# Two feed-forwards whose activations are turned by the DMA: another order of writes in the copy ahead of it, and a later place for the transposes

## The chip, the cores and the metric

The kernel runs on one core of one Trainium2 chip. The metric is the device time of an execution in microseconds; the number to compare is the median of the runs. One execution is also recorded by the profiler, and every figure of a trace below is from that one.

## The reference, cut to what matters

A block of two layers on 256 tokens of width 2048, in float32: layer 0 mixes with differential attention, layer 1 with a state-space scan, and each ends in a gated feed-forward of 5,632 hidden columns, modulated by a vector made from `c`.

```python
for i in range(DEPTH):                     # DEPTH = 2
    ada = c_act @ ada_w[i] + ada_b[i]      # shift, scale and gate, twice
    ...
    x = x + gate1 * m                      # m: attention (layer 0) or scan (layer 1)
    h = rms_norm(x, norm2_g[i]) * (1.0 + scale2) + shift2
    x = x + gate2 * swiglu(h, ffn_w_gate_up[i], ffn_w_down[i])

def swiglu(h, w_gate_up, w_down):
    g, u = jnp.split(h @ w_gate_up, 2, axis=-1)
    return (jax.nn.silu(g) * u) @ w_down
```

The change is in what lies between the two products of `swiglu`: silu(g) * u comes out with tokens on the partitions, and the second product needs hidden columns there, so it must be transposed.

## The kernel before, in words

**Units.** Weights are read from HBM once, in units of 256 rows by 512 columns (512 KB). `split_unit` (line 249) issues a unit's load on SP's queue into one of seven buffers `raw` (L253), ScalarE (ACT) casts it to `wh`, the high part (L256), and VectorE (DVE) subtracts to get `wl`, the low part. TensorE (PE) then does 12 matmuls of 512 columns: two 128-row tiles, two blocks of 128 tokens, three products of high and low parts. There are four buffers of `wh` and `wl`, so the cast of a unit waits for PE to finish the unit four before it, and the load for a `raw` buffer that the subtraction has freed. The helper that records PE's and DVE's instructions has line 120 in all rows.

**Order.** Nothing reorders instructions: each engine and each queue runs them as the program writes them. `push_unit` puts a unit's products into a first-in, first-out list, up to four units behind the loads; when a unit is taken out, its products are written, and then `tick` (line 198) lets other work advance. That work is in generators in the list `active`; `step_all` (line 179) runs each to its next `yield`, once per unit, so a `yield` is a distance of one unit. `flush_steps` (line 221) runs them all to their ends at once.

**Jobs.** The modulation vectors of later stages are computed beside all this: a job loads 512 KB of `ada_w` into the same seven `raw` buffers (L436), and DVE multiplies and adds it into `acc`. In layer 0's feed-forward 0.65 to 0.7 jobs are started per unit; in layer 1's there are hardly any in the second half of the first product.

**The feed-forward** (`ffn`, line 1328) goes in chunks j = 0 to 10 of 512 hidden columns, a gate and an up half each. Of chunks 0 to 4 and of chunk 5's up half the first half of the rows was summed and put aside in tiles `part` before the second half of the input was known. From then on a chunk takes 8 units (chunks 5, 0, 1, 2, 3 and 4, in that order; 4 for the gate, 4 for the up half) and then 16 (chunks 6 to 10). When an up half is done, `up_done` (line 1369) multiplies it on DVE into `sg`, one tile of 128 tokens by 512 columns for each of two blocks b, and starts `rest`:

- `halfwords` (L368): ACT takes each 4-byte word of `sg` apart into its two 2-byte halves, low halves in the tile's first 512 places, high halves in the second. Its loop runs over the words and within one over the halves, so that the writes go to and fro between the two places, 1,024 bytes apart.
- `turn` (L374): a DMA issued by SP transposes that tile, 128 partitions by 1,024 halves.
- `words` (L379): ACT puts the turned halves together again, in order of the result, in the tile `aT` that the second product reads. I call this the words copy.

There are 22 chunks in the two layers and two blocks in each, so 44 of each of these. The chain through `rest` is written unit by unit: one copy, a unit later the other, two units later both transposes, four units later the first words copy. Since SP issues loads and transposes from one queue, what stands behind a transpose waits while it waits for its copy.

After chunk 10 comes the down-projection, 88 units; ahead of its third column chunk, four units in, `call(flush_steps)` empties the generators (line 1468), what is left of chunk 10's `rest` among them.

Of the kernel before, what the change touches and what calls it, by code (L numbers as in the profile page):

```python
# [15 lines left out]
U16 = mybir.dt.uint16  # L16
# [14 lines left out]
RAW_BUFS = 7  # L31
W_BUFS = 4
RIPE = 1
PACE = 4
N_EARLY = 6
EPI = 3
# [55 lines left out]
def block_kernel(ctx: ExitStack, tc: tile.TileContext, x, x_t, columns_in, ssd_columns, da_columns, ada_w, ada_b,  # L92
# [13 lines left out]
    pe, act, dve, pool, sp = nc.tensor, nc.scalar, nc.vector, nc.gpsimd, nc.sync  # L106
# [65 lines left out]
        free[what] += n  # L172

    active = []
    pending = deque()
    gap = {"n": 0}
    hurry = []

    def step_all():
        for g in list(active):  # L180
            if next(g, StopIteration) is StopIteration:
                active.remove(g)
        gap["n"] -= 1
        if pending and gap["n"] <= 0 and pending[0][0]():
            _, g, n = pending.popleft()
            gap["n"] = n
            if next(g, StopIteration) is not StopIteration:
                active.append(g)
# [9 lines left out]
    def tick():  # L198
        while ripe and ripe[0][0] <= 0:
            ripe.popleft()[1]()  # L200
        for r in ripe:
            r[0] -= 1
        ada["acc"] = min(ada["acc"] + ada["rate"], 4.0)
        for k in ("dve", "dma"):
            load[k] = max(load[k], load["pe"] - 4000.0)
        while ada["acc"] >= 1.0 and len(jobs) > ada.get("floor", 0) and room():
            jobs.popleft()()
            ada["acc"] -= 1.0
        if not jobs:
            ada["acc"] = 0.0  # L210
        step_all()
# [9 lines left out]
    def flush_steps():  # L221
        while active or pending:
            step_all()

    def step_until(gen):
        while gen in active:
            step_all()
# [136 lines left out]

    def halfwords(src, p):

        h = p.tile([128, 2, 512], U16, tag="halfwords", name="halfwords", bufs=3)
        act.copy(h.rearrange("p e f -> p f e"), src.bitcast(U16).rearrange("p (f e) -> p f e", e=2))  # L368
        return h

    def turn(h, p):

        t = p.tile([128, 8, 128], U16, tag="turned", name="turned", bufs=3)
        sp.dma_start_transpose(t, h.rearrange("p e f -> p (e f)"))  # L374
        return t

    def words(dst, t):

        act.copy(dst.bitcast(U16).rearrange("p k (t e) -> p k t e", e=2),  # L379
                 t.rearrange("p (e k) t -> p k t e", e=2))  # L380
# [42 lines left out]
    def ada_job(layer, vec, finish, gate=False, halves=(0, 1)):  # L423
# [3 lines left out]
        def unit(hf, k):  # L427
            def run():
# [9 lines left out]
                def use():  # L438
# [7 lines left out]
                    if k == last:  # L446
                        acc = st["acc"]
                        ripe.append([1, lambda: finish(acc, hf)])
                ripe.append([RIPE, use])
            return run  # L450
# [84 lines left out]
    class Norm:  # L535
# [26 lines left out]
        def finish(self, b, q, on_act=False, later=False):  # L562

            ps = self.ps.pop((b, q))
            hm = tmp("hm")
            if q not in self.whole:
                self.whole[q] = act_tiles()
                self.h[q] = blocks(self.whole[q])
            h, l = self.h[q][b]
            hm3 = hm.rearrange("p (k t) -> p k t", k=4)  # L570
            for a in range(2):
                for i in (2 * a, 2 * a + 1):
                    k = 4 * q + i
                    o, p = hm3[:, i, :], ps[:, i * 128:(i + 1) * 128]
                    if on_act:
                        act.activation(o, p, AF.Identity, bias=self.Tm[:, k:k + 1], scale=self.S[:, k:k + 1])
                    else:
                        dve.tensor_scalar(o, p, self.S[:, k:k + 1], self.Tm[:, k:k + 1],
                                          op0=ALU.mult, op1=ALU.add)
            for a in range(2):  # L580
                k2 = slice(2 * a, 2 * a + 2)
                act.copy(h[:, k2, :], hm3[:, k2, :])

            def low():
                for a in range(2):
                    k2 = slice(2 * a, 2 * a + 2)
                    dve.tensor_tensor(l[:, k2, :], hm3[:, k2, :], h[:, k2, :].bitcast(F32), op=ALU.subtract)
            if later:
                return low
            low()  # L590
# [561 lines left out]
    for hg in range(4):  # L1152
        for qb, heads in ((0, (0, 1, 2, 3)), (1, (0, 1)), (1, (2, 3))):
            pending.append((lambda hg=hg: index[hg, 0] in ready and index[hg, 1] in ready,
                            attend(hg, qb, heads), PACE))

# [171 lines left out]
    def ffn(layer, end, first_jobs, final):  # L1328
        key = f"f{layer}"
        st = {}  # L1330
        top, low = ExitStack(), ExitStack()
# [13 lines left out]
        def slot(i, name):  # L1345

            return st["top" if i < 5 or i == 10 else "low"].tile([128, 4, 256], F32, tag=f"slot{i}", name=name)
# [21 lines left out]
        def up_done(j, bk, sg, i=None):  # L1369
            for b in range(2):  # L1370
                u = bk()[b]
                if i is not None:
                    dve.tensor_tensor(part[i][b], u, part[i][b], op=ALU.add)
                    u = part[i][b]
                dve.tensor_tensor(sg[b], sg[b], u, op=ALU.mult)

            def rest():
                yield
                turned = []
                for b in range(2):  # L1380
                    turned.append(halfwords(sg[b], st["top"]))
                    yield
                yield
                turned = [turn(h, st["top"]) for h in turned]
                for _ in range(4):
                    yield
                t = slot(10 if j == 5 else j if j < 5 else j - 1, f"aT_{j}")
                for b in range(2):
                    words(t[:, :, b * 128:(b + 1) * 128], turned[b])
                    yield  # L1390
                aT[j] = t
            active.append(rest())

        hl = {}

# [30 lines left out]
        sg = []  # L1426
        call(lambda bk=bk, sg=sg: gate_done(bk, sg))
        call(lambda: ada.update(rate=FFN_RATES[layer][1]))
        for i, (j, v) in [(10, (5, 1))] + list(enumerate(lead))[:10]:
            bk = Banks()  # L1430
            norm.push(wgu, v * F + j * 512, 512, bk, qs=(2, 3))
            if v == 0:
                sg = []
                call(lambda bk=bk, sg=sg, i=i: gate_done(bk, sg, i))
            else:
                call(lambda j=j, bk=bk, sg=sg, i=i: up_done(j, bk, sg, i))
        call(lambda: ada.update(rate=len(jobs) / 70))
        for j in range(6, 11):
            sg = []
            bk = Banks()  # L1440
            norm.push(wgu, j * 512, 512, bk)
            call(lambda bk=bk, sg=sg: gate_done(bk, sg))
            bk = Banks()
            norm.push(wgu, F + j * 512, 512, bk, after=(lambda: split(0)) if j == 10 else None)
            call(lambda j=j, bk=bk, sg=sg: up_done(j, bk, sg))
            if layer == 0 and j in (6, 8):
                call(ssd_load if j == 6 else ssd_finish)
# [488 lines left out]
```

## Time and profile before

| | us |
|---|---|
| median of 3 runs (2706.62 to 2714.54) | 2706.7 |
| the profiled execution's own time | 2713.09 |
| its span in the trace | 2711.4 |
| PE busy | 2637.8 |
| DVE busy | 1946.9 |
| ACT busy | 1574.1 |
| 44 copies at L368 | 214.9 |

The page gives busy time by engine, the costliest groups of instructions with the idle time ahead of them and what ended it, and the chain of work that ended last. "Busy" on PE counts a matmul from its start to its end while the next one is already in the array, so a start-to-start distance in the timeline says more of PE's pace than its busy share. In a table by stretch the granted clock is that of TensorE, with 1.00 for full speed. SPq is SP's queue, from which nearly all loads are issued.

### The profile page before, as it was taken

The page shows a single profiled execution, that of the slowest core. Times are in us where ns is not written, and L with a number is a line of the kernel's source. Part 1 is how long each engine was busy: PE and PEld are TensorE (multiplying, and loading weights), DVE is VectorE, ACT ScalarE, POOL GpSimd, SP SyncE. Part 2 cuts the span into 40 slices and gives each one's busy share as a digit, 9 for nine tenths or more (in the row PEclk, how much of TensorE's full clock was granted, in tenths as well). Part 3 has the DMA queues.
Part 4 walks back from the last instruction along what each step waited for, and adds up shares of the span by engine and source line. Part 5 has one row for each costly group of instructions (what it writes and reads, how often), then busy time and mean ns, then how long its engine had stood idle before and what let it go on. Part 6 is the DMA issues. An engine that isn't in the chain of part 4 may idle for free.

```text
span 2711.4 us, 35573 instructions
## 1 busy us (share of the span) xinstructions
PE 2637.8 (97%) x13072; PEld 2172.1 (80%) x13072; DVE 1946.9 (72%) x2263; ACT 1574.1 (58%) x1978; POOL 202.0 (7%) x205
## 2 busy tenths in 40 slices
PE   8999999999889999999999999999999999999999
PEld 4667778788667777888999989988888777887887
DVE  6778888777677876777777777776687554446776
ACT  4356754556765665445646566565545787666443
POOL 0024320001001210001000010010000000000001
PEclk9999999999999999999999999999999999999999
DMA  9977788698789987885566666666687555747885
GB/s 394 382 278 241 270 284 316 251 313 296 263 288 330 312 329 247 286 287 193 173 219 228 213 235 233 211 229 190 194 330 283 166 179 190 253 157 266 294 288 185
DMA packets 240464, 696.60 MB, mean 257 GB/s; under 512 B 68785, under 2 KB 77345, under 8 KB 239009
## 3 DMA queue, kind: packets, MB, share of 16 engines
q1 hardware_dynamic: 238560, 692.47, 72.7%
q8 instruction: 102, 1.67, 0.3%
q0 software_dynamic: 864, 1.62, 0.2%
q14 instruction: 74, 0.60, 0.1%
q10 hardware_dynamic: 864, 0.24, 0.0%
HBM read 680.52 MB, written 2.19 MB: 252 GB/s over the span
## 4 chain that ended last, share of the span: by engine, by line
PE 75%; DMA 7%; ACT 7%; DVE 6%; issue 4%; POOL 1%; SPq 0%; ACTq 0%; DVEq 0%; POOLq 0%
PE mm L120 58%; PE wk L120 13%; DMA raw<-in_ffn_w_gate_up 6%; PE po L120 4%; ACT halfwords L368 3%; ACT wh L256 3%; DVE wl L120 2%; DVE acc L120 2%; DVE sg L120 0%; DMA raw<-in_ffn_w_down 0%; DVE res L120 0%; DVE x L120 0%; DMA araw<-in_ada_w 0%; DMA raw<-in_ssd_w_in 0%; DMA cw<-in_ssd_columns 0%
## 5 line engine op out<-in xcount | busy, mean ns | idle before, releaser
L256 ACT CAST wh<-raw 128x1024 fp32r<-128x1024 f32 (+2 forms) x894 | 936.5, 1055 | 945.1 <-PE mm L120 517.7
L120 DVE TENSOR_TENSOR wl<-raw,wh 128x1024 fp32r<-128x1024 f32 (+2 forms) x894 | 1097.2, 1237 | 496.4 <-ACT wh L256 493.3
L120 PE MATMUL mm<-wh,ah 128*128 128x512 f32 (+1 forms) x2560 | 1021.1, 399 | 22.9 <-ACT wh L256 16.3
L120 PE MATMUL mm<-wl,ah 128*128 128x512 f32 (+1 forms) x2560 | 1008.6, 394 | 23.3 <-DVE wl L120 22.6
L120 PE MATMUL mm<-wh,al 128*128 128x512 f32 (+1 forms) x2560 | 1003.4, 392 | 0.1
L120 PEld LDWEIGHTS mm<-wh,ah 128*128 128x128 f32 x2560 | 484.2, 189 | 157.1 <-ACT wh L256 27.8
L120 PEld LDWEIGHTS mm<-wl,ah 128*128 128x128 f32 x2560 | 484.9, 189 | 140.0 <-DVE wl L120 42.9
L120 PEld LDWEIGHTS mm<-wh,al 128*128 128x128 f32 x2560 | 484.3, 189 | 102.1 <-DVE al L120 1.4
L120 DVE SCALAR_TENSOR_TENSOR acc<-raw,cT,acc 128x1024 f32<-128x1024 f32 x300 | 384.1, 1280 | 0.4
L368 ACT COPY halfwords<-sg 128x1024 uint16<-128x1024 uint16 x44 | 214.9, 4884 | 1.4 <-DVE sg L120 1.4
L120 PE MATMUL wk<-wl,ah 128*128 128x512 f32 x360 | 140.3, 390 | 1.3 <-DVE wl L120 1.3
L120 PE MATMUL wk<-wh,ah 128*128 128x512 f32 x360 | 140.2, 389 | 0.0
L120 PE MATMUL wk<-wh,al 128*128 128x512 f32 x360 | 140.1, 389 | 0.0
L120 PE MATMUL mm<-ah,wh 128*128 128x256 f32 x720 | 118.8, 285 | 0.0
L120 PE MATMUL mm<-al,wh 128*128 128x256 f32 x720 | 117.7, 283 | 0.0
L120 PE MATMUL mm<-ah,wl 128*128 128x256 f32 x720 | 117.6, 283 | 0.0
L530 POOL PARTITION_ALL_REDUCE gate<-acc x12 | 41.4, 3491 | 953.1 <-DVE acc L120 946.5
L120 PEld LDWEIGHTS mm<-ah,wh 128*128 128x128 f32 x720 | 100.2, 192 | 0.1
L120 PEld LDWEIGHTS mm<-ah,wl 128*128 128x128 f32 x720 | 100.2, 192 | 0.0
L120 PEld LDWEIGHTS mm<-al,wh 128*128 128x128 f32 x720 | 100.2, 192 | 0.0
L120 PEld LDWEIGHTS wk<-wl,ah 128*128 128x128 f32 x360 | 67.6, 188 | 16.2 <-DVE wl L120 2.2
L120 PEld LDWEIGHTS wk<-wh,ah 128*128 128x128 f32 x360 | 67.6, 188 | 14.2 <-ACT wh L256 0.3
(308 smaller groups left out, 2068.7 us busy)
## 6 DMA issues: line engine op xcount, KB each, us to landing
raw<-in_ffn_w_gate_up SPq DMA_DIRECT2D x352, 512.0 KB, 5.4
raw<-in_ada_w SPq DMA_DIRECT2D x320, 512.0 KB, 5.2
raw<-in_ffn_w_down SPq DMA_DIRECT2D x176, 512.0 KB, 5.1
raw<-in_ssd_w_in SPq DMA_DIRECT2D x136, 512.0 KB, 4.6
raw<-in_da_w_in SPq DMA_DIRECT2D x90, 512.0 KB, 5.3
araw<-in_ada_w SPq DMA_DIRECT2D x64, 512.0 KB, 8.5
raw<-in_ssd_w_out SPq DMA_DIRECT2D x64, 512.0 KB, 4.4
raw<-in_da_w_out SPq DMA_DIRECT2D x32, 512.0 KB, 5.3
```

The lines of the kernel that those rows point to most:

```text
L120: return fn(dst, *a, **k)
L256: act.copy(wh[:, at, :n], raw[:, at, :n])
L368: act.copy(h.rearrange("p e f -> p f e"), src.bitcast(U16).rearrange("p (f e) -> p f e", e=2))
L530: pool.partition_all_reduce(mods["G", key][:, o:o + 512], acc[:, i * 512:(i + 1) * 512], 128, ReduceOp.add)
```

## The change

Three things are different.

1. `halfwords` writes its tile in order: first all 512 low halves, then all 512 high ones. It reads every other half of `sg` for that. The same halves end in the same places.
2. `rest` lets six units (`LOADS_AHEAD`) pass after the second copy, then issues the transposes one by one, a unit apart, and two units later the words copies. From copy to transpose it was two units; it is now seven from either copy to its own transpose. From a transpose to its words copy it stays four. `halfwords` and `turned` have four buffers each for three.
3. `rest` is put into a list of its own, `apart`. `step_all` steps it after `active`, but `flush_steps` no longer runs until it is empty.

```diff
+LOADS_AHEAD = 6
...
     def step_all():
-        for g in list(active):
-            if next(g, StopIteration) is StopIteration:
-                active.remove(g)
+        for gs in (active, apart):
+            for g in list(gs):
+                if next(g, StopIteration) is StopIteration:
+                    gs.remove(g)
...
-        h = p.tile([128, 2, 512], U16, tag="halfwords", name="halfwords", bufs=3)
-        act.copy(h.rearrange("p e f -> p f e"), src.bitcast(U16).rearrange("p (f e) -> p f e", e=2))
+        h = p.tile([128, 2, 512], U16, tag="halfwords", name="halfwords", bufs=4)
+        act.copy(h, src.bitcast(U16).rearrange("p (f e) -> p e f", e=2))
...
-        t = p.tile([128, 8, 128], U16, tag="turned", name="turned", bufs=3)
+        t = p.tile([128, 8, 128], U16, tag="turned", name="turned", bufs=4)
...
             def rest():
                 yield
+                halves = []
+                for b in range(2):
+                    halves.append(halfwords(sg[b], st["top"]))
+                    yield
+                for _ in range(LOADS_AHEAD):
+                    yield
                 turned = []
-                for b in range(2):
-                    turned.append(halfwords(sg[b], st["top"]))
+                for h in halves:
+                    turned.append(turn(h, st["top"]))
                     yield
-                yield
-                turned = [turn(h, st["top"]) for h in turned]
-                for _ in range(4):
+                for _ in range(2):
                     yield
...
-            active.append(rest())
+            apart.append(rest())
```

Lines 368, 374, 379, 253, 256, 359 and 436 of before are 371, 377, 382, 256, 259, 362 and 439 after it.

SP's queue in layer 0, at the first transposes (chunk 5). Before:

```order
L436 DMA raw<-in_ada_w 128x1024
L253 DMA raw<-in_ffn_w_gate_up 128x1024
L436 DMA raw<-in_ada_w 128x1024
L253 DMA raw<-in_ffn_w_gate_up 128x1024
L374 DMA_TRANSPOSE turned<-halfwords 128x8x128 x2
L253 DMA raw<-in_ffn_w_gate_up 128x1024
```

After, from the same job on:

```order
L439 DMA raw<-in_ada_w 128x1024
L256 DMA raw<-in_ffn_w_gate_up 128x1024
L439 DMA raw<-in_ada_w 128x1024
L256 DMA raw<-in_ffn_w_gate_up 128x1024 x2
L439 DMA raw<-in_ada_w 128x1024
L256 DMA raw<-in_ffn_w_gate_up 128x1024
L439 DMA raw<-in_ada_w 128x1024
L256 DMA raw<-in_ffn_w_gate_up 128x1024 x2
L439 DMA raw<-in_ada_w 128x1024
L256 DMA raw<-in_ffn_w_gate_up 128x1024
L439 DMA raw<-in_ada_w 128x1024
L377 DMA_TRANSPOSE turned<-halfwords 128x8x128
L256 DMA raw<-in_ffn_w_gate_up 128x1024
L377 DMA_TRANSPOSE turned<-halfwords 128x8x128
```

The first transpose stands five weight loads and four jobs further on, and a weight load stands between the two.

ACT in layer 0, from the second copy of chunk 10 on, into the down-projection. Before:

```order
L368 COPY halfwords<-sg 128x512x2
L256 CAST wh<-raw 128x1024 x2
L379 COPY aT_8758<-turned 128x4x256 x2
L256 CAST wh<-raw 128x1024 x6
L359 CAST ah<-aT_6725 128x512 x2
```

After:

```order
L371 COPY halfwords<-sg 128x1024
L259 CAST wh<-raw 128x1024 x8
L362 CAST ah<-aT_6839 128x512 x2
L259 CAST wh<-raw 128x1024 x3
L382 COPY aT_8958<-turned 128x4x256
L259 CAST wh<-raw 128x1024
L382 COPY aT_8958<-turned 128x4x256
```

The words copies of the last chunk stood two casts behind their copy and together; now the first stands eleven casts behind it. On PE, DVE and POOL no instruction moves.

More of the change, by code (lines that the diff above doesn't have):

```diff
@@ L174, in block_kernel @@
     active = []
+    apart = []
     pending = deque()
```

## The prediction

> **What bounds the kernel now.** The page comes first: TensorE is busy nearly throughout, so at most its idle time and its slow time can be won, and one ACT group stands out: 44 copies of 4.9 us each.
>
> ```profile
> PE 2637.8 (97%) x13072; PEld 2172.1 (80%) x13072; DVE 1946.9 (72%) x2263; ACT 1574.1 (58%) x1978; POOL 202.0 (7%) x205
> L368 ACT COPY halfwords<-sg 128x1024 uint16<-128x1024 uint16 x44 | 214.9, 4884 | 1.4 <-DVE sg L120 1.4
> ```
>
> A busy PE is not a fast PE, so the second view is the table by stretch. Its columns are stretch: length, busy us and count of PE, PEld, DVE, ACT and POOL, the granted clock, the DMA share, GB/s.
>
> ```profile
> 520.00:650.00 130.00, 130.00 (x598) 108.13 (x598) 100.22 (x100) 67.41 (x88) 0.00 (x0) 1.00 0.90 321
> 655.00:795.00 140.00, 126.11 (x509) 98.45 (x508) 97.60 (x99) 107.12 (x72) 15.67 (x8) 0.95 0.80 271
> 795.00:1035.00 240.00, 225.27 (x957) 178.54 (x956) 179.94 (x153) 149.60 (x118) 30.76 (x16) 0.99 0.86 304
> 1050.00:1240.00 190.00, 190.00 (x840) 157.36 (x839) 145.01 (x126) 87.50 (x93) 12.29 (x4) 1.00 0.85 301
> 2125.00:2252.00 127.00, 120.59 (x512) 96.25 (x511) 66.58 (x70) 107.68 (x72) 0.00 (x0) 0.99 0.55 186
> 2252.00:2475.00 223.00, 220.11 (x954) 179.12 (x953) 105.36 (x94) 146.55 (x116) 0.00 (x0) 0.99 0.58 204
> ```
>
> Stretches 1 and 4 have no halfwords copy and lose nothing: 840 matmuls in 190 us. Those between (layer 0, then layer 1) hold all 44 copies, and there PE does 509 in 140 us, the clock falls to 0.95 and ACT is busy 107 of 140 us. The full pace, from the PE timeline, is 16 matmuls from the first row below to the second: 3.63 us, 0.227 us each, 2.72 us for a unit of 12. The other rows are one stall: 1.43 and 0.76 us of idle, then matmuls 0.42 us apart.
>
> ```profile
> 659.87 0.39 PE L120 MATMUL mm<-wh,ah 128*128 128x512 f32 x1
> 663.50 0.39 PE L120 MATMUL mm<-wl,ah 128*128 128x512 f32 x1
> ...
> 691.75 0.50 PE L120 MATMUL mm<-wh,ah 128*128 128x512 f32 x1 [1.43 <-ACT wh L256]
> 693.01 0.63 PE L120 MATMUL mm<-wl,ah 128*128 128x512 f32 x1 [0.76 <-DVE wl L120]
> 693.43 0.63 PE L120 MATMUL mm<-wh,al 128*128 128x512 f32 x1
> ```
>
> The loss is the distance between copies that stand a known number of units apart (ACT's timeline, the first copy of chunks 5, 4 and 10 in each layer): 40 units from the first to the second, 80 from the second to the third.
>
> ```profile
> 652.87 4.92 ACT L368 COPY halfwords<-sg 128x1024 uint16<-128x1024 uint16 x1
> 790.00 4.87 ACT L368 COPY halfwords<-sg 128x1024 uint16<-128x1024 uint16 x1
> 1028.64 4.89 ACT L368 COPY halfwords<-sg 128x1024 uint16<-128x1024 uint16 x1
> 2123.15 4.88 ACT L368 COPY halfwords<-sg 128x1024 uint16<-128x1024 uint16 x1
> 2246.34 4.90 ACT L368 COPY halfwords<-sg 128x1024 uint16<-128x1024 uint16 x1
> 2468.03 4.88 ACT L368 COPY halfwords<-sg 128x1024 uint16<-128x1024 uint16 x1
> ```
>
> At 2.72 us a unit, 40 units are 108.8 us and 80 are 217.6. Layer 0 took 137.1 and 238.6, so it lost 28.3 and 21.0; layer 1 took 123.2 and 221.7 and lost 14.4 and 4.1. After the last pair the backlog is emptied at once, in 25 us each:
>
> ```profile
> 1030.00:1055.00 25.00, 23.34 (x100) 18.19 (x99) 12.11 (x15) 18.57 (x14) 0.00 (x0) 1.00 0.62 209
> 2468.00:2493.00 25.00, 23.35 (x100) 18.31 (x99) 11.66 (x12) 19.87 (x14) 0.00 (x0) 1.00 0.56 187
> ```
>
> 100 matmuls are worth 22.7 us, so 2.3 is lost in each. **All told 72.4 us** lie around these copies: 49.3 + 18.5 + 4.6.
>
> Why PE waits is in the groups of 655 to 795 and in the waits of SP's queue:
>
> ```profile
> L368 ACT COPY halfwords<-sg 128x1024 uint16<-128x1024 uint16 x11 | 53.6, 4876 | 0.0
> L120 DVE TENSOR_TENSOR wl<-raw,wh 128x1024 fp32r<-128x1024 f32 x40 | 48.7, 1222 | 40.8 <-ACT wh L256 40.5
> L256 ACT CAST wh<-raw 128x1024 fp32r<-128x1024 f32 x41 | 46.0, 1134 | 28.0 <-DMA raw<-in_ffn_w_gate_up 24.9 <-DVE sg L120 2.7 <-PE mm L120 0.4
> L120 DVE SCALAR_TENSOR_TENSOR acc<-raw,cT,acc 128x1024 f32<-128x1024 f32 x25 | 32.0, 1279 | 0.0
> L379 ACT COPY aT<-turned 128x1024 uint16<-128x1024 uint16 x10 | 11.7, 1168 | 0.0
> ...
> L1366 ACT ACTIVATE sg<-sg 128x512 f32<-128x512 f32 x10 | 6.3, 631 | 4.9 <-DVE sg L120 4.8
> ```
>
> ```profile
> SPq L253 <- DVE wl L120: 978.7, 533, 14.6
> ...
> SPq L374 <- ACT wh L256: 300.0, 43, 14.9
> ```
>
> ```profile
> 685.24 6.87 SPq L374 DMA_TRANSPOSE turned<-halfwords  x2
> 692.20 1.01 SPq L253 DMA_DIRECT2D raw<-in_ffn_w_gate_up  x2
> ```
>
> Two things meet. ACT is full: for 40 units the casts, copies, words copies and Silus take 46.0 + 53.6 + 11.7 + 6.3 = 117.6 us, against PE's 108.8. And SP stands at the transposes until the copy is done (300.0 us at 43 of them), so no load is issued from 685.24 to 692.20 and ACT, the copies behind it, waits for weights (24.9 us).
>
> **The change part by part.** *Writes in order.* No row shows a copy that reads every other half and writes a run. The nearest is the words copy: 1,024 halves, gathered from two places 1,024 bytes apart and written as a run, 1.17 us. The form it replaces also reads 1,024 halves but writes alternately to two places 1,024 bytes apart, 4.88. The difference between the two is the order of the writes, so I take 1.17; bounds 1.13 (the cast of 1,024 elements in these groups) and 4.88. 44 x (4.88 - 1.17) = 163 us of ACT time go. For 40 units ACT then needs 46.0 + 11 x 1.17 + 11.7 + 6.3 = 77 us of 108.8. The 163 us are no gain in themselves; what counts is PE's 72.4.
>
> *Transposes later.* The 44 transposes and their bytes stay; each now stands between loads, five and six units further on. In layer 0, SP cannot be as far ahead as that: seven raw buffers at 1.6 loads a unit (25 job rows, acc, beside 40 of wl) are 4.3 units. In layer 1, with hardly a job (186 GB/s for 127 us are 23.6 MB, 45 tiles of 0.52 beside 40 units, transposes included), seven buffers are seven units, so a wait of one copy, about 1.2 us a pair, can stay; PE has four prepared units, 10.9 us, over it. So of the 300.0 us of waiting I expect under 25, and loads flow. The SP time of a transpose, 1.24 us, and its landing, 3.1, are as before; the third row is ACT's wait for turned tiles, in all:
>
> ```profile
> L374 SPq DMA_TRANSPOSE turned<-halfwords x44: 1232/1243/1532, 657.9 to 2479.6; - x44
> ...
>   ACT aT L379: 0.5, 2
> ...
> DMA to landing us min/median/max: 3.0/3.1/6.7
> ```
>
> The words copies still stand four units (10.9 us) behind the transposes on ACT, so even a landing of 6.7 is covered. Behind them on ACT are the casts: if that cover were gone, they would wait.
>
> *The list of its own, and four buffers.* The emptying before the down-projection's third chunk no longer runs through the last pair, so the 4.6 us go with it. The fourth buffers hold two chunks in flight; without them the copies of the next chunk would wait for a transpose. They cost nothing in time.
>
> *What is late next.* In layer 0 VectorE: 97.6 us of work stand beside 40 units, 90% of 108.8, and no lossless stretch here has it over 77% (100.2 of 130). Bounds: nothing, if it never waits; or, with the idle time it has before its subtractions in the lossless stretch 520 to 650,
>
> ```profile
> L120 DVE TENSOR_TENSOR wl<-raw,wh 128x1024 fp32r<-128x1024 f32 x47 | 57.3, 1224 | 23.6 <-ACT wh L256 23.4
> ```
>
> 0.5 us for each, 40 x 0.5 = 20 us more, 117.6, which leaves 8.8 us of the 28.3. For the 80 units that follow it is 179.9 + 40 = 219.9 against 217.6, 2.3 us. I take both upper ends, 11 us, since what stalls remain also cost slow matmuls, 0.2 us more for each. Layer 1 has 66.6 us of VectorE work for 108.8 and keeps nothing.
>
> **Sum:** 72.4 - 11 = 61 us. The profiled execution took 2713.1 us (span 2711.4), so such a one should take about 2652. It was a long one; the median of the three runs is 2706.7, and 61 less is **2645 us**. Nothing says whether the 6 us between them lie in the stalls.
>
> **A rule that differs.** The slow matmuls are given back here as part of the stall that precedes them. The Trainium skill (TensorE: Matmul & The Clock Gate, "What's actually happening") has the clock halved only after an idle window of about 3.4 us. The trace disagrees: 1.43 and 0.76 us sufficed at 691.75.
>
> **The rivals.** *A: layer 0 stays short of loads.* Seven raw buffers serve weights and jobs alike; if the late loads come of that ring and not of SP's stop at the transposes, layer 0 keeps its second loss (21.0) and half its first (14.2). For it: SP waits 978.7 us at loads for a subtraction to free a buffer. Against it: 520 to 650 runs at 321 GB/s with the same ring and loses nothing. Gain 72.4 - 35.2 = 37: 2670.
>
> *B: the copy stays at 4.9 us* because reading halves is what is slow. Against it speaks the words copy. ACT would be full in the first 40 units of each layer (117.6 against 108.8 leaves 8.8 in each, 17.6); with the later losses (21.0 + 4.1) halved, 12.5, the gain is 42: 2665.
>
> *C: the clock dips are not the stalls' doing*, which is what the rule above would mean here: 140 x 0.05 + (240 + 127 + 223) x 0.01 = 12.9 us would stay, 2658. Against it: every lossless stretch has 1.00.
>
> *D: slower.* The words copies wait on ACT for late transposes, and the casts behind them with them. It decides when a transpose lands over 10.9 us after its place, that is when SP is 4.2 us behind with a landing of 6.7. Each of 22 pairs then costs its excess; to end over 8 us slower than before, 80 us of new stalls, 3.7 us a pair, a landing 14.6 us after its place: 2716. Against it are ACT's 0.5 us in all before.
>
> *E: nothing moves*, because the stalls have a common cause elsewhere: 2707. Layer 1, with the same loads and hardly a job, loses 14.4 us exactly where the copies stand close; that is against it.
>
> **How the numbers follow.** Chances: forecast 0.70, A 0.12, B 0.06, C 0.05, D 0.03, E 0.04. What a measurement can tell here is 0.3%, 8 us: faster 0.93, same 0.04, slower 0.03. Lower end: all 72.4 won, 2634. The forecast's own upper end is the whole of VectorE's price twice, 2656; the range goes on to just past A, 2672, with which under 2 in 10 are left out.
>
> **What would show it.** Copies at about 1.2 us; SP's waits at the transposes under 25 us; about 108.8 to 118 and 218 to 220 us between the marked copies; clock 1.00; ACT waiting for PE instead of for loads. It is wrong if the copies stay near 4.9, if ACT waits for turned tiles, or if layer 0 keeps over 20 us.

## The result, and the profile after

The median fell from 2707.0 to 2641.4 us (6 runs each; 2706.4 to 2714.5 and 2639.4 to 2643.2). The ratio is 0.9752, with a 95% interval of 0.974 to 0.9765. The profiled execution took 2643.2 us with a span of 2641.5, 69.9 us less than the one before.

TensorE (PE) first, from the page: its busy time fell by 31 us while the span fell by 70, so 39 us of idle time went and 31 us in which matmuls stood in the array longer than they need.

```profile
PE 2606.6 (99%) x13072; PEld 2167.3 (82%) x13072; DVE 1951.3 (74%) x2263; ACT 1415.9 (54%) x1978; POOL 204.9 (8%) x205
```

The ACT timeline has the marked copies (chunks 5, 4 and 10 of each layer), now 1.04 us long:

```profile
651.32 1.04 ACT L371 COPY halfwords<-sg 128x1024 uint16<-128x1024 uint16 x1
760.97 1.03 ACT L371 COPY halfwords<-sg 128x1024 uint16<-128x1024 uint16 x1
979.78 1.04 ACT L371 COPY halfwords<-sg 128x1024 uint16<-128x1024 uint16 x1
2074.49 1.04 ACT L371 COPY halfwords<-sg 128x1024 uint16<-128x1024 uint16 x1
2183.29 1.04 ACT L371 COPY halfwords<-sg 128x1024 uint16<-128x1024 uint16 x1
2400.89 1.04 ACT L371 COPY halfwords<-sg 128x1024 uint16<-128x1024 uint16 x1
```

From first to second and second to third they stand 109.65 and 218.8 us apart in layer 0, 108.8 and 217.6 in layer 1. Forty and eighty units at the full pace of 2.72 us are 108.8 and 217.6. So layer 1 loses nothing, and layer 0 has 0.85 and 1.2 us left of 28.3 and 21.0. The table by stretch (length, busy us and count of PE, PEld, DVE, ACT and POOL, the granted clock, the DMA share, GB/s) says the same and shows what is close to its limit instead; its last two rows are the 25 us after the last pair of copies in each layer:

```profile
651.30:761.00 109.70, 109.70 (x484) 90.26 (x483) 98.66 (x99) 65.52 (x70) 17.36 (x8) 1.00 1.02 333
761.00:979.80 218.80, 218.80 (x965) 180.33 (x964) 182.84 (x154) 115.22 (x119) 31.63 (x16) 1.00 0.96 344
2074.50:2183.30 108.80, 108.80 (x482) 90.09 (x481) 67.45 (x70) 65.42 (x70) 0.00 (x0) 1.00 0.79 218
2183.30:2400.90 217.60, 217.60 (x962) 180.18 (x961) 105.06 (x92) 112.57 (x116) 0.00 (x0) 1.00 0.70 206
2400.00:2425.00 25.00, 25.00 (x112) 20.71 (x111) 15.27 (x14) 12.83 (x14) 0.00 (x0) 1.00 0.84 257
979.00:1004.00 25.00, 25.00 (x112) 20.43 (x111) 15.43 (x16) 12.56 (x14) 0.00 (x0) 1.00 0.82 240
```

PE is busy in every one and the clock is 1.00, where it was 0.95 to 0.99 between the old copies. VectorE (DVE) has 98.7 us of work beside 109.7 and the DMA engines are full, and PE hardly waits for either. In the first 40 units of layer 0 ACT's casts now wait more for PE than for loads (first row, groups of 651 to 761). In the 80 units after them they still wait mostly for loads, 70.9 us (second row, 761 to 979.8), and nearly all of it is hidden from PE. SP's queue hardly stops at a transpose (the waits of SP's queue), and the transposes land later than before (the view of the tile `turned`):

```profile
L259 ACT CAST wh<-raw 128x1024 fp32r<-128x1024 f32 x41 | 43.2, 1054 | 45.4 <-PE mm L121 32.7 <-DMA raw<-in_ffn_w_gate_up 7.5 <-ACT halfwords L371 2.3
L259 ACT CAST wh<-raw 128x1024 fp32r<-128x1024 f32 x81 | 85.4, 1054 | 104.0 <-DMA raw<-in_ffn_w_gate_up 70.9 <-PE mm L121 28.4 <-DVE wl L121 4.6
```

```profile
SPq L377 <- PE mm L121: 1.3, 1, 1.3
```

```profile
L377 SPq DMA_TRANSPOSE turned<-halfwords x44: 1231/1626/3572, 666.8 to 2416.3; - x44
...
DMA to landing us min/median/max: 4.2/5.8/10.6
```

### The profile page after: what moved, and what is told of

Read it like the earlier page. It is cut to its first block, busy times and chain, and to the rows that moved or that the text cites. A ratio compares the mean times of both kernels' runs of the same rounds, so it can differ in the third digit from the quotient of the medians.

```text
span 2641.5 us, 35533 instructions
## 1 busy us (share of the span) xinstructions
PE 2606.6 (99%) x13072; PEld 2167.3 (82%) x13072; DVE 1951.3 (74%) x2263; ACT 1415.9 (54%) x1978; POOL 204.9 (8%) x205
## 4 chain that ended last, share of the span: by engine, by line
PE 93%; DVE 3%; ACT 1%; DMA 1%; issue 1%; POOL 1%; SPq 0%; ACTq 0%; POOLq 0%; DVEq 0%
PE mm L121 75%; PE wk L121 14%; PE po L121 4%; DVE wl L121 1%; ACT wh L259 1%; DVE acc L121 0%; DMA raw<-in_ssd_w_in 0%; DVE res L121 0%; DMA araw<-in_ada_w 0%; DVE x L121 0%; DMA raw<-in_da_w_in 0%; ACT hm L579 0%; DMA raw<-in_da_w_out 0%; DVE hm L121 0%; ACT e L1078 0%
## 5 line engine op out<-in xcount | busy, mean ns | idle before, releaser
L259 ACT CAST wh<-raw 128x1024 fp32r<-128x1024 f32 (+2 forms) x894 | 925.1, 1040 | 1039.0 <-PE mm L121 642.8
L121 PE MATMUL mm<-wl,ah 128*128 128x512 f32 (+1 forms) x2560 | 997.3, 390 | 1.3 <-DVE wl L121 1.3
L121 PEld LDWEIGHTS wk<-wh,al 128*128 128x128 f32 x360 | 67.6, 188 | 14.0
```

Of the source, the lines that this page charges most:

```text
L121: return fn(dst, *a, **k)
L259: act.copy(wh[:, at, :n], raw[:, at, :n])
```

## The experiments

All are built on the kernel before or on the changed one, and each computes the whole result. Times are medians; "lost" is the distance between the marked copies less 108.8 or 217.6 us.

### One part alone

The copy in order in the kernel before:

```diff
-        act.copy(h.rearrange("p e f -> p f e"), src.bitcast(U16).rearrange("p (f e) -> p f e", e=2))
+        act.copy(h, src.bitcast(U16).rearrange("p (f e) -> p e f", e=2))
```

> The kernel before with the copy's writes in order alone; transposes at their old place, three buffers, one list. Two-causes theory (a full ACT and SP's stop at the transposes both make PE wait): the copy takes 1.04 us as in the changed kernel, SP still waits at the transposes, about 300 - 44 x 3.8 = 130 us or more in all, and some of the 72 us stays: 2650 to 2670 us. ACT-alone rival (SP's stop is hidden by the four prepared units once ACT has time): as the changed kernel, 2641 plus at most 6 us, although SP waits over 100 us. SP-alone rival (the late loads are the cause): over 2685 us.

Measured: 2645.9 us, ratio 0.9769 (0.9755 to 0.9784). The copy alone has nearly all of the gain, as the ACT-alone rival said. SP still stops at the transposes for 167 us, and it is hidden:

```profile
SPq L374 <- ACT wh L256: 87.7, 20, 12.2
SPq L374 <- ACT halfwords L368: 79.5, 21, 10.2
```

The later transposes, with the old copy in the changed kernel (the same two lines the other way round; the list of its own and the fourth buffers stay):

> The changed kernel with the old copy (writes to and fro, 4.9 us); transposes late, four buffers, list of its own. Two-causes theory: SP's waits at the transposes go (under 25 us), ACT stays full in the first 40 units of each layer (117.6 us of work for 108.8), 8.8 us kept in each and half of the later losses: about 2665 us, between 2655 and 2680. ACT-alone rival: 2695 to 2707, hardly better than before. SP-alone rival: 2641 to 2650.

Measured: 2673.6 us, ratio 0.9875 (0.986 to 0.989), inside the range of the two-causes theory, but with other shares than it gave. By stretch:

```profile
653.96:778.35 124.39, 116.93 (x494) 92.69 (x493) 94.99 (x98) 101.07 (x70) 15.65 (x8) 0.99 0.87 289
778.35:1007.72 229.37, 221.19 (x954) 178.89 (x953) 182.40 (x155) 150.57 (x118) 33.92 (x16) 0.99 0.92 331
2101.60:2212.07 110.47, 110.28 (x482) 89.88 (x481) 64.09 (x68) 100.73 (x69) 0.00 (x0) 1.00 0.71 210
2212.07:2430.45 218.38, 218.31 (x961) 179.63 (x960) 106.17 (x95) 147.32 (x114) 0.00 (x0) 1.00 0.63 207
```

Layer 0 still loses 15.6 and 11.8 us; layer 1 only 1.7 and 0.8, though its copies are as slow as ever. ACT alone, which fitted the first run, is refuted by this one (it asked for 2695 or more), and the two causes as I had them, each for a share of its own, by the first. In layer 1 either remedy is enough: a slow copy is hidden if the loads keep coming, and late loads are hidden if the copy is quick. The two parts win 62 and 34 us alone and 66 together: they remove the same stalls.

Why does the same old copy cost layer 0 so much more than layer 1? In this run's first 40 units of each layer the casts stand idle for different things (groups of 654 to 778.3, layer 0, and of 2101.6 to 2212, layer 1):

```profile
L259 ACT CAST wh<-raw 128x1024 fp32r<-128x1024 f32 x41 | 45.7, 1130 | 20.1 <-DMA raw<-in_ffn_w_gate_up 16.2 <-DVE sg L121 2.3 <-PE mm L121 1.7
L259 ACT CAST wh<-raw 128x1024 fp32r<-128x1024 f32 x41 | 45.0, 1125 | 6.4 <-PE mm L121 6.4
```

In layer 1 ACT waits for PE, so it is as far ahead as the four buffers allow when a pair of copies begins. In layer 0 it waits 16.2 us for loads, which share their seven buffers with the jobs, so a pair begins with less prepared. No run takes the jobs out of layer 0, so that step is read from the trace and not tested.

No run gives late transposes three buffers either, so what the fourth are worth is not shown.

### Is the later place worth anything once the copy is quick?

Changed kernel and copy alone again, five and four executions on one chip.

> The changed kernel, unaltered, for a comparison with the next run on one chip: 2641 us, within 3.

> The writes in order alone, as in the first experiment. If the later transposes are worth something once the copy is quick: 3 to 6 us slower than the changed kernel, all of it in layer 0, where SP still stops at the transposes. If the 4 us between the medians of the first comparison were chance: within 1.5 us of it.

Measured: 2643.5 us (2641.9 to 2645.2; ratio 0.9759, 0.9745 to 0.9772) for the changed kernel, 2647.2 (2641.5 to 2648.6; 0.9768, 0.9755 to 0.9782) for the copy alone. The medians are 3.7 us apart, much as in the first comparison (2645.9 and 2641.4), but the intervals overlap. The traces agree in where it lies: the copy alone lost 1.9 and 5.6 us in layer 0 in this run's trace (1.9 and 3.5 in the first), against 0.85 and 1.2, and in both nothing over the whole of layer 1. Probably 3 to 4 us, then; the timing by itself doesn't prove it.

### The list of its own

```diff
-            apart.append(rest())
+            active.append(rest())
```

> The changed kernel with the generators of the activations in the common list again, so that the emptying ahead of the down-projection's third column chunk runs the last chunk's transposes and words copies in a burst. If the 2.3 us lost there in each layer came of the burst: 4 to 5 us slower than the changed kernel, with ACT waiting 3 us or more for a turned tile in each layer. If they came of the 4.9 us copies: within 1.5 us of the changed kernel.

Measured: 2642.7 us, 1.3 above the changed kernel, and full 25 us stretches after the last copies:

```profile
984.00:1009.00 25.00, 25.00 (x112) 20.43 (x111) 15.35 (x16) 14.69 (x17) 0.00 (x0) 1.00 0.83 295
2402.00:2427.00 25.00, 25.00 (x112) 20.72 (x111) 15.10 (x14) 14.97 (x17) 0.00 (x0) 1.00 0.80 283
```

Behind quick copies the burst does no harm. Slow copies are not the whole of the 4.6 us lost there before either: with them, late transposes and the list of its own, the run above does 108 and 106 matmuls in such 25 us, where 112 is full and 100 were done before, and so still loses about 1.5.

### What makes a copy slow

```diff
+RUNS = [512, 512, 512, 512, 512, 512, 1, 2, 4, 8, 16]
...
+            act.copy(h.rearrange("p e (o i) -> p o e i", i=run),
+                     src.bitcast(U16).rearrange("p (o i e) -> p o e i", i=run, e=2))
```

> The changed kernel with other loop orders in the copy of chunks 6 to 10 of each layer: the writes go in runs of 1, 2, 4, 8 and 16 halves before they change between the two places; the values written are the same. From 4.88 us with runs of one and 1.04 us without changes, a change of place costs 3.75 ns if each costs the same: runs of 2, 4, 8, 16 take 2.96, 2.00, 1.52, 1.28 us. If a half written alone is what costs and a pair (a 4-byte word) is written as fast as anything: 1.0 to 1.3 us from runs of 2 on. If lines of 16 bytes matter: 2.9 us or more up to runs of 4, and near 1.1 from 8 on.

The ACT timeline, one copy each with runs of 1, 2, 4, 8 and 16 halves:

```profile
804.88 4.90 ACT L375 COPY halfwords<-sg 128x1024 uint16<-128x1024 uint16 x1
852.11 1.17 ACT L377 COPY halfwords<-sg 128x1024 uint16<-128x1024 uint16 x1 [1.42 <-DVE sg L122]
895.07 1.04 ACT L377 COPY halfwords<-sg 128x1024 uint16<-128x1024 uint16 x1
940.42 1.04 ACT L377 COPY halfwords<-sg 128x1024 uint16<-128x1024 uint16 x1
982.12 1.04 ACT L377 COPY halfwords<-sg 128x1024 uint16<-128x1024 uint16 x1
```

A half written alone, with its neighbour elsewhere, costs 4.8 ns; two neighbours in a row bring the copy to 1.17 us, four to the full pace. So it is not each change of place that costs, nor each change of a 16-byte line, or runs of 2 and 4 would cost as much as the expectation says; what costs is a half without a neighbour. Whether a neighbour helps because the two make up one 4-byte word, or only because they lie close together, the run does not tell: no run writes two halves that are near but not side by side. The whole took 2643.5 us in its one run.

### How much of ACT's time PE can bear

The changed kernel, with each in-order copy made several times over:

```diff
-        act.copy(h, src.bitcast(U16).rearrange("p (f e) -> p e f", e=2))
+        for _ in range(5):
+            act.copy(h, src.bitcast(U16).rearrange("p (f e) -> p e f", e=2))
```

> The changed kernel with each copy in order made five times over (the same values to the same place): some 4.9 to 5.2 us of ACT for each half-chunk, as the old copy takes, but with no half written alone. It is to tell why the late transposes with the old copy keep 15.6 us of loss in the first 40 units of layer 0, 11.8 in the 80 after them, and 1.7 and 0.8 in layer 1. If ACT's time alone is what counts: about as much, 10 to 20 and 7 to 15 in layer 0, under 5 in layer 1, about 2668 to 2680 us. If the scattered writes also held up VectorE or another engine at the memory: under 5 us in each stretch, about 2645 to 2655.

Its one execution took 6744 us: matmuls were 0.6 us apart (499.29, 499.91, 500.40, 501.02 and so on) from the start, a thousand microseconds ahead of the first copy. So it was made again, and with four and three copies:

> The same program as e5, whose one execution had matmuls 0.6 us apart from its first microseconds on, far ahead of the first copy. If that was the execution and not the edit, the pace is 0.227 us again and the expectations of e5 stand: with ACT's time alone counting, 10 to 20 us lost in the first 40 units of layer 0 and 7 to 15 in the 80 after, 2668 to 2680 us; with scattered writes that hold up other engines, under 5 us in each, 2645 to 2655. If it was the edit, over 6000 us again.

> As the run with five copies, with four. In the run with five, a group takes 5.27 us of ACT's time from its start to the next instruction's, where the old copy takes 4.40 (it overlaps its neighbours at both ends); four copies should take 4.2. If ACT's time alone is what counts, this run lies a little under the one with the old copy and late transposes (2673.6): 2664 to 2674 us. If the scattered writes of the old copy cost something besides: under 2660.

> With three copies, 3.15 us of ACT's time, 6.3 for a pair, well inside the 10.9 us that PE has prepared. If the loss sets in when ACT as a whole runs out of time (here 46 + 33 + 12 + 6 = 97 us of 109 for 40 units, and less for the overlap): nothing lost, 2640 to 2647 us. If each microsecond of ACT time costs in proportion (30 us lost at 4.40, 54 at 5.27, none at 1.04): 12 to 22 us lost, 2653 to 2664.

The pace was the usual one again. The same place in the ACT timelines of the old copy with late transposes, and of five, four and three copies (a pair of copies, the cast between them and the two behind):

```profile
728.04 4.92 ACT L371 COPY halfwords<-sg 128x1024 uint16<-128x1024 uint16 x1
732.44 1.38 ACT L259 CAST wh<-raw 128x1024 fp32r<-128x1024 f32 x1
733.71 4.89 ACT L371 COPY halfwords<-sg 128x1024 uint16<-128x1024 uint16 x1
738.08 2.31 ACT L259 CAST wh<-raw 128x1024 fp32r<-128x1024 f32 x2
```

```profile
733.40 5.36 ACT L372 COPY halfwords<-sg 128x1024 uint16<-128x1024 uint16 x5
...
744.87 1.99 ACT L259 CAST wh<-raw 128x1024 fp32r<-128x1024 f32 x2
```

```profile
699.40 4.28 ACT L372 COPY halfwords<-sg 128x1024 uint16<-128x1024 uint16 x4
703.58 1.05 ACT L259 CAST wh<-raw 128x1024 fp32r<-128x1024 f32 x1
704.54 4.27 ACT L372 COPY halfwords<-sg 128x1024 uint16<-128x1024 uint16 x4
708.71 2.00 ACT L259 CAST wh<-raw 128x1024 fp32r<-128x1024 f32 x2
```

```profile
697.72 3.20 ACT L372 COPY halfwords<-sg 128x1024 uint16<-128x1024 uint16 x3
...
704.88 2.00 ACT L259 CAST wh<-raw 128x1024 fp32r<-128x1024 f32 x2
```

From the start of the pair to the end of the third cast:

| copy | us for pair and casts | lost in layer 0 (40, 80 units) | lost in layer 1 | median us |
|---|---|---|---|---|
| three in order | 9.2 | 2.4, 0.5 | 0, 0 | 2644.4 |
| four in order | 11.3 | 9.9, 7.8 | 0, 0 | 2660.1 |
| old, to and fro | 12.4 | 15.6, 11.8 | 1.7, 0.8 | 2673.6 |
| five in order | 13.5 | 20.6, 19.7 | 7.2, 6.4 | 2701.8 |

The old copy stands in this row where its time puts it. Each stretch has five pairs, so what PE bears of a pair is its time less a fifth of the loss. In layer 1 that is 12.0 us in the first 40 units, from the old copy and from five in order alike, and 12.2 in the 80 after; four in order, 11.3, lies below it and loses nothing. In layer 0 it is 9.2 to 9.3 in the first 40 units, from four, old and five, and 9.5 to 10.0 in the 80 after. Scattered and in-order writes give the same figures, so ACT's time is enough to explain the loss: ACT falls behind by what a pair takes beyond what is prepared. By count of the buffers that is four units, 10.9 us; layer 1 bore somewhat more, and layer 0, where the casts wait for loads, less.

The copy expected beside the old one, four, fell just below its range (2660 for 2664 to 2674), at the edge of the rival's "under 2660", because the copy's own 4.40 us isn't all: next to it a cast starts 1.27 us ahead of what follows, where it is 0.96 beside in-order copies. Whether that third of a microsecond is the scattered writes still draining was not tried.

### Is VectorE the next bound?

```diff
+                for _ in range(1 if layer == 0 and i is not None else 0):
+                    dve.tensor_tensor(sg[b], sg[b], sg[b], op=ALU.max)
```

> The changed kernel with one more VectorE instruction per half-chunk in the first 40 units of layer 0 (sg becomes the larger of sg and sg, the same values; 0.65 us each, 10 of them, 6.5 us): VectorE then has about 105 us of work beside 109.7 us of matmuls, 96%. If VectorE needs the idle time that the prediction charged (0.5 us a unit), the stretch between the copies of chunks 5 and 4 grows from 109.7 to about 125 us. If it can run full as long as PE has four units prepared: 109 to 112 us.

> As the run before it with three such instructions, 19.5 us: about 118 us of VectorE work beside 109.7 us of matmuls, 108%. If VectorE can run full, it is the bound now: the stretch takes 116 to 122 us and PE stalls. With the idle time charged in the prediction: about 138 us. If VectorE had nothing to do with the end at all: 109 to 111 us.

The first stretch with one instruction more, and with three:

```profile
653.90:763.50 109.60, 109.60 (x483) 90.23 (x482) 107.22 (x109) 65.42 (x69) 19.02 (x8) 1.00 1.01 334
```

```profile
654.80:780.10 125.30, 114.76 (x485) 92.28 (x484) 120.69 (x128) 66.19 (x70) 20.49 (x8) 0.97 0.91 291
```

At 107.2 us of VectorE work in 109.6, 98%, PE loses nothing (2643.6 us in one run). At 120.7 it is the bound: 125.3 us, 3 more than expected, with PE stalls of up to 4.3 us and a clock of 0.97 (2662.7 us).

## Why the prediction was right

The time came 3.6 us below the 2645 forecast, inside the range. Some of that nearness is luck: the gain in the trace was 9 us more than the 61 forecast, and 4.3 of these are missing in the median only because the profiled execution before was a long one.

**The loss of 72.4 us** was the right quantity: 70.4 of it went (27.5 + 19.8 + 14.4 + 4.1 between the copies, 4.6 after them), and the span fell by 69.9. The median fell by less, 65.6; the prediction had left open whether its long profiled execution was long in the stalls. (The stretches said to hold all 44 copies hold the starts of 41; three begin just outside, and nothing hangs on it.)

**The copy** takes 1.04 us, not the 1.17 of the words copy, and less than the lower bound of 1.13. That bound came from casts of which some stood next to old copies; the casts in the same stretch take 1.05 now. The words copy reads alternately from two places, which may be what its 0.13 us more are for. The Trainium skill (ScalarE: Activation LUTs, "What ACT_TABLE_LOAD costs") gives 186 ns and 0.833 ns for each element for an ACTIVATE with immediate scale and bias, 1.04 us by estimate for 1,024; this copy's row (1.04) agrees, and the words copy's (1.17) does not.

**What stays, 11 us**, was the mis-sized term. The step charged VectorE 0.5 us of idle time a unit, taken from a stretch in which it had less to do (77%). It measured 2.1 us, and the run with 98% shows that VectorE needs no idle time while PE has four units prepared. It binds between 98% and 110%.

**The two causes** were right together, but their shares were not. I called ACT full because busy times came to 117.6 us for 40 units. Instructions overlap their neighbours, so a sum over groups counts time twice: the table's own row for that stretch has ACT busy for 107.1 us, and it holds 11 copies where 40 units have 10. With the old copies at late transposes layer 1 did 40 units in 110.5 us with ACT busy for 100.7. What was full was not ACT over 40 units but what PE has prepared when a pair begins, against 12.4 us for a pair and its casts: 12.0 to 12.2 in layer 1, where SP's stop had to be added before PE waited long, and 9.2 to 10.0 in layer 0. And SP's stop, the other cause, probably costs only 3 to 4 us once the copy is quick. Rival B's 8.8 us a layer was wrong accordingly (15.6 and 1.7), and its 2665 came out as 2673.6.

**SP's waits** at the transposes fell from 300.0 us to 1.3, where I had allowed 25. That the transposes' landing would stay at 3.1 us was wrong: 5.8, at most 10.6. The four units between a transpose and its words copy still covered it; ACT waited for no turned tile. Rival D had its point of decision at 10.9 us, closer than I thought.

**The list of its own** was credited with the 4.6 us after the last copies. The run without that list wins them too, so behind quick copies the list isn't needed, and the step named the wrong cause for the right sum.

**Rivals A, C and E** fell: layer 0 keeps 2.1 us, and the clock is 1.00 in every stretch of the table. The slow clock went with the stalls, and came back with them in the run with three extra VectorE instructions (0.97). A was right that layer 0 stays short of loads: in its 80 units the casts wait 70.9 us for them, and the sign that ACT would wait for PE instead fails there. Its price was wrong, as quick copies leave PE enough prepared to hide that.

## What to carry to other kernels

Work out what a burst on a serial engine takes against what the bound engine has prepared when the burst begins, not the engine's share of a long stretch: bursts of 9.2 us cost 3 us in all, bursts of 12.4 cost 30. Where loads come late, less is prepared than the buffers allow. Two changes that remove the same stall don't add up (62 and 34 made 66), so try each alone before both are kept. When 2-byte data must be scattered, put the loop so that at least two neighbours are written in a row; reading apart costs little.

## What was not expected of the hardware

ACT writes 2-byte elements singly at 4.8 ns each, against 1.0 in runs of four or more: 4.90 and 1.04 us for 1,024. A run of two already takes 1.17.

The DMA transposes land in 5.8 us (median) where they took 3.1, now that loads are in flight beside them (DMA share 1.02 in 109.7 us, 0.80 before). The share is not all: with the copy alone, at a share of 1.00 in the same 40 units, they land in 4.3, and at the later place with the old copy, at 0.87, in 6.0. SP's time for issuing one rose from 1.24 to 1.63 in this trace, but is 1.25 with four copies at the same places.

One execution ran all its matmuls about 0.6 us apart and took 6744 us, while the same program took 2698 to 2705 in eight others. Nothing in its trace says why.
